# Hybrid encoder layer on one core: gate tiles stored from ScalarE's queue, a fourth row buffer, one rotary scratch per engine, and branch B's table arithmetic placed in a later phase

## The chip, the core and the metric

The kernel runs on one core of one Trainium2 chip. The metric is device microseconds of one execution, the median of several runs; lower is better. The core's engines are TensorE (PE in the profile), VectorE (DVE), ScalarE (ACT), GpSimd (POOL) and SyncE (SP). Each works through its own list of instructions in order and waits on semaphores. SP's list here holds only transfers (DMAs): it issues each one when its condition holds, and everything behind it on the list waits for that.

## The reference

One layer of an encoder, applied to two request groups (prompt and sample, 1024 tokens each, model width 1024) with the same weights:

```python
mod = silu(c) @ w_ada + b_ada;  shift, scale, gate = split(mod, 3)
h = rms_norm(x, norm_g) * (1 + scale) + shift
qa, ka, va, za, qb, kb, vb, zb, ga, gb = split(h @ w_in, ...)
# branch A: 8 q heads, 2 kv heads, width 64, RMSNorm of q and k, axial rotary positions
oa = gqa_attention(rope(norm(qa)), rope(norm(ka)), va) * silu(za)
# branch B: 4 heads, two softmax maps each, lambda from lam_q1, lam_k1, lam_q2, lam_k2
ob = rms_norm(diff_attention(rope16(norm(qb)), rope16(norm(kb)), vb, lam), subln_g) * (1 - lam_init)
pa = oa @ w_proj_a;  pb = (ob * silu(zb)) @ w_proj_b
merged = sigmoid(ga) * pa + sigmoid(gb) * pb
y = x + gate * (merged @ w_out)
```

Everything is float32.

## The kernel before, in words

Matrices are multiplied as high and low halves: `split_w` copies a weight tile into `w`'s high half on ACT (L209) and the difference into its low half on DVE (L210), and each product is three matmuls. The layer runs once for the prompt (group 0, the first 975 us or so) and once for the sample (group 1).

In each group the combined projection is cut in streams, written as Python generators: `kva_gen` (keys and values of A), `qa_gen` (queries of A, two halves), `vb_gen` and `qkb_gen` (branch B), and `z_gen`, which makes the gate paths: per 128 x 512 tile 24 matmuls (L900), a tanh from the PSUM bank into the single buffer `ev` (`z_out`, L882), and a store of `ev` to DRAM (L887). Tiles of za and zb are "gated": DVE forms silu in `ev` (L884) before the store. Tiles of ga and gb, 32 of the 48 in each group, are not. Because `ev` has one buffer, the next tile's tanh waits until the store has landed.

Rows of q and k (128 tokens) go through `rows`: ACT copies PSUM into a `row` buffer (`rtile`, three of them) and squares it, DVE sums, POOL takes the power. `rope` turns them: cos product into a scratch `rc` (L728; one buffer for both engines), two sin products (L737), a sum that reads `rc` (L738). `by_turns` gives even tiles to DVE and odd ones to POOL while `alone` or `easy` holds, else all to POOL. `pairs_T` transposes the rows on PE (L749) and evacuates the bank by ACT (L751) and DVE (L752).

Attention runs in steps: scores (L927 and L928) into one of two double banks, maximum on DVE (L929), exponential on ACT (L931), transposition of 32 x 32 blocks on DVE (L972), four SP transfers that finish it (`q<-p`, L977), and the product with V (L1003 in A, L1040 in B). `swapped` loads the turned halves of q (`sw<-u`, L783).

`weave` sets the order in which the streams are written down: it always takes the stream whose done share, less a constant, is least. The shares and constants are the tables at the top (`ATT_W`, `IN_A`, `Z_A`, `GATE_A`, `FIRST_A`, `Z_FIRST_A`, `LATE_A`). A scheduler then places the instructions on the engines by priority; `dma_next` and `in_order` keep the order of the program.

Group 0's head computes modulation, normalised input and first projections. `gate_gen` forms the adaLN gate in two halves (its matmuls on L110 read `cpad`, in the `at` scratch; ACT L625, PE L629, DVE L631). When the head is done, `load_tables_B` loads the rotary tables of branch B, its gains, the four lambda vectors and `subg`, and does all arithmetic on them (L581 to L600) before the first attention is written down. At a group's end `gated_gen` loads a piece of attention output and of z into two `row` buffers (L1146, L1147), multiplies them (L1152 or L1156, L1160) and splits the product (L1161, L1162); then come `merge_gen` (L1189 matmuls) and `out_gen` (L1220 matmuls).

Of the kernel before, what the change touches and what calls it, by code (L numbers as in the profile page):

```python
# [20 lines left out]
P = 128  # L21
T = 1024
D = 1024
NCH = D // P
NTT = T // P
HD = 64
EPS = 1e-6
LAM_INIT = 0.8 - 0.6 * math.exp(-0.3 * 0)
# [12 lines left out]
Z_HEAD = (7, 6)  # L41
Z_HEAD_A = (-0.216, -0.32)
ATT_W = (
    (0.733, 1.008, 0.894, 1.192, 1.03, 1.769),
    (1.237, 1.862, 1.041, 1.418, 0.645, 1.256),
)
IN_A = (
    (0.044, -0.07, 0.861, 0.05, 0.25, 0.15),
    (0.125, -0.05, 0.368, 0.3, -0.03, 0.694),
)  # L50
Z_A = (
    (0.2, 0.05, 0.62, -0.05, -0.1, -0.05),
    (-0.215, 0.07, 0.2, 0.16, -0.3, -0.1),
)
LAST_ATT = (46, 40)
LAST_FILL = (20, 25)
GATED_A = (0.063, -0.144)
LATE_A = 1.202
EARLY_A = 0.9
QUARTER_P = 202  # L60
KV_STEPS = 12
GATE_A = (-0.778, -0.677)
FIRST_ATT = 12
FIRST_A = 0.357
TAIL = (3, 3)
TAIL_A = (0.92, 1.2)
# [47 lines left out]
def kernel(ctx: ExitStack, tc: tile.TileContext, t: dict):  # L114
    nc = tc.nc
    ent = ctx.enter_context

    const = ent(tc.tile_pool(name="const", bufs=1))
# [47 lines left out]
    def ptile():  # L166
        return ppool.tile([P, 1024], F32, tag="p", name=nm("p"))
# [10 lines left out]
    def mtile(tag, shape, dt=F32, bufs=None):  # L178
        return mpool.tile(shape, dt, tag=tag, name=nm(tag), bufs=bufs)

    def rtile():
        return mtile("row", [P, 512], bufs=3)

    dma = nc.sync.dma_start
    act, vec, pe = (in_order(tc, e) for e in (nc.scalar, nc.vector, nc.tensor))
# [101 lines left out]

    ccol = const.tile([P, NCH, 2], F32, name="ccol")  # L290
    bcol = const.tile([P, 3, NCH], F32, name="bcol")
    gcol = const.tile([P, NCH], F32, name="gcol")
# [167 lines left out]

    def start(ht):
        still = rtile()[:, :256]
        nc.vector.memset(still, 0.0)
        cpad = mtile("at", [P, 256], bufs=1).rearrange("p (c m) -> p c m", c=NCH)
        nc.vector.memset(cpad, 0.0)
        nc.scalar.activation(cT, ccol, AF.Tanh, scale=0.5)
        nc.vector.scalar_tensor_tensor(out=cT, in0=cT, scalar=1.0, in1=ccol, op0=ALU.add, op1=ALU.mult)
        nc.vector.tensor_scalar(out=cT, in0=cT, scalar1=0.5, scalar2=None, op0=ALU.mult)
        nc.vector.tensor_copy(cpad[:, :, :2], cT)
        xT = [load_xT0(0)]  # L470
        wts = [load_ada(n) for n in range(2)]
# [24 lines left out]
        rsb = spread(rs, pe)
        idle(WARM[3], still[:, :128])
        vec.tensor_scalar(out=bcol[:, 1, :], in0=bcol[:, 1, :], scalar1=1.0, scalar2=None, op0=ALU.add)
        part = ada_part(ada_half(wts[1], cpad, 1, first))
        early.update({n: four_sums() for n in range(2)})  # L500
        ps = ada_sum(part)
        idle(WARM[4], still[:, :128])
        with tc.high_priority(offset=QUARTER_P):
            for quarter in range(4):
                cs = range(quarter * 2, quarter * 2 + 2)
                if quarter % 2 == 0:
                    add_h(ht, 0, quarter // 2)
# [12 lines left out]
                for c in cs:  # L520
                    sums_early(ht, c, 0)
                part = ada(wts[quarter * 2 + 2 : quarter * 2 + 4], cpad) if quarter < 3 else None
                for c in cs:
                    sums_early(ht, c, 1)
                    if part is not None:
                        ps, part = ada_sum(part), None
        kva_w.append((drain_last(z_first),))
        sq = late_squares(xT[1])
        return lambda: inv_rms(sq, pe), lambda rs: start_late(ht, xT[1], rs), gate_gen(cpad)
# [14 lines left out]
            if c % 2:  # L544
                yield 1

    cosB = const.tile([P, 2, NTT, 16], F32, name="cosB")
    sinB = const.tile([P, 2, NTT, 16], F32, name="sinB")
    gqa = const.tile([P, HD], F32, name="gqa")
    gka = const.tile([P, HD], F32, name="gka")  # L550
# [19 lines left out]
    def load_tables():  # L570
        for dst, src in ((gqa, "qn_a"), (gka, "kn_a")):
            dma_next(dst, t[src][0].partition_broadcast(P))
        nc.vector.tensor_scalar(out=gqa, in0=gqa, scalar1=SC, scalar2=None, op0=ALU.mult)

    def load_tables_B():
        for dst, src in ((cosB, "cosB"), (sinB, "sinB")):
            for a in range(2):
                dma_next(dst[:, a], t[src].rearrange("(n p) d -> p n d", p=P))
        for i, src in enumerate(("qn_b", "kn_b")):
            dma_next(gB[:, i, :], t[src][0].partition_broadcast(P))  # L580
        nc.vector.tensor_scalar(out=gB[:, 0, :], in0=gB[:, 0, :], scalar1=SC, scalar2=None, op0=ALU.mult)  # L581
        for a in range(2):
            by_q(cosB[:, a], sinB[:, a], gB[:, a], 8)

        nc.vector.tensor_tensor(out=gB[:, 0, 16:], in0=gB[:, 0, 16:], in1=gB[:, 1, 16:], op=ALU.mult)

        lamw = ptile()
        lamv = lamw[:, : 4 * HD].rearrange("p (a d) -> p a d", a=4)
        for i, src in enumerate(("lam_q1", "lam_k1", "lam_q2", "lam_k2")):
            dma_next(lamv[:, i, :], t[src][0].partition_broadcast(P))  # L590
        lamp = lamw[:, 4 * HD : 6 * HD].rearrange("p (a d) -> p a d", a=2)
        nc.vector.tensor_tensor(
            out=lamp, in0=lamv[:, 0::2, :], in1=lamv[:, 1::2, :], op=ALU.mult
        )
        nc.vector.tensor_reduce(out=lam2, in_=lamp, axis=AX.X, op=ALU.add)
        nc.scalar.activation(lam2, lam2, AF.Exp)
        nc.vector.tensor_tensor(out=nlam, in0=lam2[:, 1:2], in1=lam2[:, 0:1], op=ALU.subtract)
        nc.vector.tensor_scalar(out=nlam, in0=nlam, scalar1=-LAM_INIT, scalar2=None, op0=ALU.add)
        dma_next(subg, t["subln_g"].rearrange("o e -> e o"))
        nc.vector.tensor_scalar(out=subg, in0=subg, scalar1=0.5 * (1.0 - LAM_INIT) * math.sqrt(2 * HD), scalar2=None, op0=ALU.mult)  # L600

    def load_tables_A(st):

# [113 lines left out]
    def rope(x3, s3, cos, sin, half, e):  # L717

        nh, w = x3.shape[1], x3.shape[2]
        c3 = mtile("rc", [P, 4, HD], bufs=1)[:, :nh, :w]  # L720
        k, g = cos.shape[1], w // (2 * half)
        if k == 1:
            cs = cos.to_broadcast([P, nh, w])
# [156 lines left out]
    def z_out(dst, key, ps, gated):  # L880
        ev = mtile("ev", [P, 512], bufs=1)
        nc.scalar.activation(ev, ps, AF.Tanh, scale=0.5)  # L882
        if gated:
            nc.vector.scalar_tensor_tensor(out=ev, in0=ev, scalar=1.0, in1=ps, op0=ALU.add, op1=ALU.mult)  # L884
        dt = dpool.tile([P, 512], F32, name=nm("zd"))
        dst[key] = dt
        dma(dt, ev)  # L887

    def z_gen(ht, col, dst, i0, gated, w=None, hfs=(0, 1)):
        w = w or load_w(w_cols(w_in, (col, 256)))  # L890
# [131 lines left out]
    def b_values(u):  # L1022
# [20 lines left out]
        else:  # L1043
# [6 lines left out]
                pv(*ready.pop(0))  # L1050
                yield 1
            pv(*ready.pop())
        sq = mtile("at", [P, 256], bufs=1)
        o = mtile("oo", [P, 256])
        nc.scalar.activation(query_order(sq), piece_order(acc), AF.Square)
        nc.vector.tensor_copy(query_order(o), piece_order(acc))
# [283 lines left out]
    for g in range(2):  # L1340
        st = states[g]
# [5 lines left out]
        zs = chain(*items)  # L1347
        qa = head(g, st, zs, late)
        alone[0] = False
        if g == 0:  # L1350
            load_tables_B()

        att = attention(units_of(st), qa)

# [8 lines left out]
        if g == 0:  # L1363
            weave((islice(att, FIRST_ATT), FIRST_ATT, 0.0), (qa, 15, FIRST_A), (islice(zs, Z_FIRST[1]), Z_FIRST[1], Z_FIRST_A[1]))
        easy[0] = True
        phase(0, qa_gen(st, 1))
        phase(1, vb_gen(ht, st["vb"], 0), qkb_gen(ht, st["qkb"], 0))
        easy[0] = False
        oT, mT = ([], []), ([], [])
# [85 lines left out]
```

## Time and profile before

| | |
|---|---|
| median of 3 runs | 1889.12 us (1887.71 to 1893.15) |
| the profiled execution | 1889.37 us, its span 1887.3 us |
| PE busy | 1853.1 us, 98% of the span |
| DVE, ACT, POOL busy | 1229.1, 845.5, 362.7 us |
| transfers | 297.51 MB, all through one queue that SP issues |

The span runs from the first to the last instruction; the 2.07 us between it and the execution's time lie outside the trace. PE's busy time counts pipelined matmuls from issue to end, so a busy PE can still be slower than it could be; idle time on PE is a loss without doubt. In a row of instructions, "[2.97 <-DVE u L752]" means that the engine stood idle for 2.97 us before it and that DVE's instruction of line 752, writing tile u, ended the wait.

### The profile page before, as it was taken

Reading aid. Unit: us, or ns where it says so; the run is one execution under the profiler, and the core shown is the slowest. Engines: PE = TensorE matmul, PEld = TensorE weight load, DVE = VectorE, ACT = ScalarE, POOL = GpSimd, SP = SyncE. Lnnn points to the kernel's source line nnn. Section 1 sums busy time; section 2 is a strip of 40 time slices with the busy share of each in tenths; the row PEclk is TensorE's granted clock in tenths of the full one; section 3 lists DMA queues with packets and bytes.
Section 4 is the critical chain, followed back from the end, with each engine's and each line's share of the span. In section 5 each row is a group of like instructions: output and inputs, shape, how many; then the busy total and the mean of one; then the engine's idle time right before and its main releaser. Section 6 shows DMA issues by size and latency. Waiting matters only on the chain.

```text
span 1887.3 us, 32062 instructions
## 1 busy us (share of the span) xinstructions
PE 1853.1 (98%) x11484; PEld 1602.5 (85%) x11484; DVE 1229.1 (65%) x1892; ACT 845.5 (45%) x1803; POOL 362.7 (19%) x692
## 2 busy tenths in 40 slices
PE   9989999999999999999999999999999999999999
PEld 7768888888889998778889888888888989877887
DVE  4746686646578678778464777666547766787731
ACT  3524454445456555424223555444445545552210
POOL 0422210011325152100124300000233513210000
PEclk9999999999999999999999999999999999999999
DMA  9525567665444436887541477766524344579532
GB/s 332 166 62 145 131 177 182 175 162 136 134 126 102 129 90 183 238 291 225 199 134 46 123 185 190 205 177 181 153 78 125 99 104 114 154 239 303 168 106 78
DMA packets 277612, 299.54 MB, mean 159 GB/s; under 512 B 37648, under 2 KB 228304, under 8 KB 277456
## 3 DMA queue, kind: packets, MB, share of 16 engines
q1 hardware_dynamic: 277456, 297.51, 55.4%
q8 instruction: 92, 1.51, 0.3%
q14 instruction: 64, 0.52, 0.1%
HBM read 137.91 MB, written 42.04 MB: 95 GB/s over the span
## 4 chain that ended last, share of the span: by engine, by line
PE 76%; DMA 7%; DVE 6%; SPq 4%; ACT 2%; POOL 2%; issue 2%; DVEq 0%; ACTq 0%; POOLq 0%
PE f L900 20%; PE f L689 19%; PE a L1003 6%; PE f L1220 5%; PE f L1189 5%; PE s L927 5%; PE s L928 5%; PE a L1040 4%; PE s L1220 4%; PE s L1189 2%; SPq L977 2%; SPq L110 2%; DMA st<-in_w_in_dram 1%; DVE m L929 1%; DMA row<-zd 1%
## 5 line engine op out<-in xcount | busy, mean ns | idle before, releaser
L900 PE MATMUL f<-u,w 128*128 128x512 f32 x2064 | 518.8, 394 | 0.9 <-ACT ev L882 0.3
L689 PE MATMUL f<-w,u 128*128 128x256 f32 x3264 | 451.3, 287 | 0.5 <-ACT ev L882 0.3
L900 PEld LDWEIGHTS f<-u,w 128*128 128x128 f32 x2064 | 379.3, 188 | 76.9 <-ACT ev L882 0.8
L689 PEld LDWEIGHTS f<-w,u 128*128 128x128 f32 x3264 | 428.0, 192 | 17.3 <-issue 0.7
L929 DVE TENSOR_REDUCE m<-s 128x1 f32<-128x1024 f32 x256 | 310.2, 1219 | 140.4 <-PE s L928 138.0
L972 DVE STREAM_TRANSPOSE p<-p 128x1024 f32<-128x1024 f32 x192 | 238.4, 1242 | 53.6 <-ACT p L931 47.8
L928 PE MATMUL s<-u,sw 128*128 128x512 f32 x512 | 202.8, 399 | 0.0
L210 DVE TENSOR_TENSOR w<-st,w 128x512 fp32r<-128x512 f32 x184 | 124.6, 707 | 88.5 <-ACT w L209 87.7
L209 ACT ACTIVATE w<-st 128x512 fp32r<-128x512 f32 x184 | 108.2, 626 | 125.1 <-DMA st<-in_w_in_dram 58.6
L931 ACT ACTIVATE p<-s,m,rsB 128x1024 f32<-128x1024 f32 x128 | 154.2, 1205 | 4.1 <-DMA q<-p 0.6
L931 ACT ACTIVATE p<-s,m,rsA 128x1024 f32<-128x1024 f32 x128 | 154.3, 1205 | 3.9 <-ACT m L930 0.4
L714 POOL TENSOR_TENSOR rsB<-ss,nhalf 128x4 f32<-128x4 f32 x64 | 66.4, 1037 | 426.2 <-DVE ss L713 415.8
L1189 PE MATMUL f<-u,w 128*128 128x512 f32 x588 | 142.5, 392 | 0.9 <-DVE u L1200 0.5
L1040 PE MATMUL a<-q,u 128*128 128x256 f32 x512 | 126.5, 390 | 7.9 <-DMA q<-p 4.6
L1189 PEld LDWEIGHTS f<-u,w 128*128 128x128 f32 x588 | 109.9, 188 | 24.5 <-DVE u L1200 0.9
L1003 PE MATMUL a<-q,u 128*64 128x128 f32 x2048 | 121.6, 277 | 3.4 <-DMA q<-p 3.4
L1003 PEld LDWEIGHTS a<-q,u 128*64 128x64 f32 x2048 | 113.0, 138 | 13.2 <-issue 6.5
L752 DVE TENSOR_TENSOR u<-f,u 64x256 fp32r<-64x256 f32 (+1 forms) x210 | 84.9, 406 | 56.2 <-ACT u L751 50.7
L1040 PEld LDWEIGHTS a<-q,u 128*128 128x128 f32 x512 | 97.4, 196 | 23.3 <-issue 5.8
L928 PEld LDWEIGHTS s<-u,sw 128*128 128x128 f32 x512 | 97.0, 189 | 16.6 <-issue 0.3
L927 PE MATMUL s<-u 128*128 128x512 f32 x256 | 107.5, 422 | 1.1 <-ACT p L931 0.9
L1220 PE MATMUL f<-u,w 128*128 128x512 f32 x456 | 105.3, 389 | 0.0
(205 smaller groups left out, 2162.7 us busy)
## 6 DMA issues: line engine op xcount, KB each, us to landing
q<-p SPq DMA_DIRECT2D x768, 128.0 KB, 2.8
st<-in_w_in_dram SPq DMA_DIRECT2D x128, 256.0 KB, 3.3
zd<-ev SPq DMA_DIRECT2D x96, 256.0 KB, 2.3
sw<-u SPq DMA_DIRECT2D x256, 64.0 KB, 2.1
p<-zd SPq DMA_DIRECT2D x64, 256.0 KB, 4.6
u<-in_w_ada_dram SPq DMA_DIRECT2D x24, 512.0 KB, 8.5
od<-oo SPq DMA_DIRECT2D x64, 128.0 KB, 2.6
st<-in_w_in_dram SPq DMA_DIRECT2D x64, 128.0 KB, 2.8
```

The source lines that it names most:

```text
L210: nc.vector.tensor_tensor(out=wl, in0=st, in1=wh.bitcast(F32), op=ALU.subtract)
L689: nc.tensor.matmul(ps, lt[c][:, sl], w[c][:, wi, :], start=(k == 0), stop=(k == 23))
L900: nc.tensor.matmul(ps, w[c][:, wi, e * P : (e + 1) * P], rt[c], start=(k == 0), stop=(k == 23),)
L927: nc.tensor.matmul(s[:, sl], q, k[:, sl], start=True, stop=False)
L928: nc.tensor.matmul(s[:, sl], sw, k[:, sl], start=False, stop=True)
L929: nc.vector.tensor_reduce(out=m, in_=s, axis=AX.X, op=ALU.max, negate=True)
L931: nc.scalar.activation(pt.rearrange("p (j c a) -> p j c a", j=4, c=8), s.rearrange("p (c a j) -> p j c a", c=8, j=4), AF.Exp, scale=rs, bi ...
L972: nc.vector.transpose(pt, pt)
L1003: nc.tensor.matmul(acc[e * 64 : e * 64 + 64, n * P : n * P + P], u["v"](k), blocks[n][:, e, k], start=(k == 0 and n == 1), stop=(k == 7 an ...
L1040: nc.tensor.matmul(acc, u["v"][:, k], pT[:, k], start=(k == 0), stop=(k == 7))
L1189: nc.tensor.matmul(ps, w[:, c, wi, d * P : (d + 1) * P], o[:, oi, :], start=(k == 0), stop=(k == 11))
L1220: nc.tensor.matmul(ps, w[c][:, wi, e * P : (e + 1) * P], m[:, mi, :], start=(k == 0), stop=(k == 23))
```

## The change

What it does, part by part:

- `z_out` issues the store of an ungated tile (ga, gb) from ACT; the gated tiles' stores stay on SP.
- `rtile` has four buffers.
- `rope` takes its scratch by engine: `rcv` on DVE, `rcg` on POOL, one buffer each. The squares of branch B's output (`sq` in `b_values`) move from `at` to `rcv`, and `at` is gone. `cpad` moves into the room of `cosB`.
- The lambda vectors are loaded in `load_tables`, into an `oo` buffer; their product and sum (`lambdas`) run with `folded`. `load_tables_B` becomes a generator: its loads are issued where they were, its arithmetic is four later steps woven into phase 0 (the second half of qa and most of A's first attention half).
- Eight constants of the weave change and TABLES_A is new; all of them bear on group 0 alone.

```diff
-    (0.733, 1.008, 0.894, 1.192, 1.03, 1.769),
+    (0.826, 1.008, 0.894, 1.192, 1.03, 1.769),        # ATT_W[0]
-    (0.044, -0.07, 0.861, 0.05, 0.25, 0.15),
+    (0.044, -0.07, 0.891, 0.05, 0.25, 0.15),          # IN_A[0]
-    (0.2, 0.05, 0.62, -0.05, -0.1, -0.05),
+    (0.099, 0.05, 0.62, -0.05, -0.1, -0.05),          # Z_A[0]
-LATE_A = 1.202
+TABLES_A = 0.0
+LATE_A = 1.25
-GATE_A = (-0.778, -0.677)
+GATE_A = (-0.778, -0.875)
-FIRST_A = 0.357
+FIRST_A = 0.073
-Z_FIRST_A = (-0.035, -0.317)
+Z_FIRST_A = (-0.093, -0.181)
...
-        return mtile("row", [P, 512], bufs=3)
+        return mtile("row", [P, 512], bufs=4)
...
-        cpad = mtile("at", [P, 256], bufs=1).rearrange("p (c m) -> p c m", c=NCH)
+        cpad = cosB.rearrange("p a n d -> p (a n d)").rearrange("p (c m) -> p c m", c=NCH)
...
+        lamv = mtile("oo", [P, 256]).rearrange("p (a d) -> p a d", a=4)
+        lams.append(lamv)
+        for i, src in enumerate(("lam_q1", "lam_q2", "lam_k1", "lam_k2")):
+            dma_next(lamv[:, i, :], t[src][0].partition_broadcast(P))
+
+    def lambdas():
+        lamv = lams.pop()
+        lamp = lamv[:, :2]
+        nc.vector.tensor_tensor(out=lamp, in0=lamp, in1=lamv[:, 2:], op=ALU.mult)
+        nc.vector.tensor_reduce(out=lam2, in_=lamp, axis=AX.X, op=ALU.add)
...
-    def load_tables_B():
+    def tables_B_gen():
...
         for i, src in enumerate(("qn_b", "kn_b")):
             dma_next(gB[:, i, :], t[src][0].partition_broadcast(P))
+        dma_next(subg, t["subln_g"].rearrange("o e -> e o"))
+        yield 1
         nc.vector.tensor_scalar(out=gB[:, 0, :], in0=gB[:, 0, :], scalar1=SC, ...)
-        for a in range(2):
-            by_q(cosB[:, a], sinB[:, a], gB[:, a], 8)
+        by_q(cosB[:, 0], sinB[:, 0], gB[:, 0], 8)
+        yield 1
+        by_q(cosB[:, 1], sinB[:, 1], gB[:, 1], 8)
         nc.vector.tensor_tensor(out=gB[:, 0, 16:], in0=gB[:, 0, 16:], in1=gB[:, 1, 16:], op=ALU.mult)
+        yield 1
+        nc.vector.tensor_scalar(out=subg, in0=subg, scalar1=..., op0=ALU.mult)
+        yield 1
         nc.scalar.activation(lam2, lam2, AF.Exp)
         nc.vector.tensor_tensor(out=nlam, in0=lam2[:, 1:2], in1=lam2[:, 0:1], op=ALU.subtract)
         nc.vector.tensor_scalar(out=nlam, in0=nlam, scalar1=-LAM_INIT, scalar2=None, op0=ALU.add)
+        yield 1
...
-        c3 = mtile("rc", [P, 4, HD], bufs=1)[:, :nh, :w]
+        c3 = mtile("rcv" if e is nc.vector else "rcg", [P, 4, HD], bufs=1)[:, :nh, :w]
...
-        dma(dt, ev)
+        (dma if gated else nc.scalar.dma_start)(dt, ev)
...
-        sq = mtile("at", [P, 256], bufs=1)
+        sq = mtile("rcv", [P, 4, HD], bufs=1).rearrange("p a d -> p (a d)")
...
             by_q(st["cosA"], st["sinA"], gqa, 16)
+            if g == 0:
+                lambdas()
...
-        if g == 0:
-            load_tables_B()
+        tables = [tables_B_gen()] if g == 0 else []
+        for gen in tables:
+            next(gen)
...
-        phase(0, qa_gen(st, 1))
+        phase(0, qa_gen(st, 1), more=[(gen, 4, TABLES_A) for gen in tables])
```

More of the change, by code (lines that the diff above doesn't have):

```diff
@@ L285, in load_w_proj @@
         return w
+    cosB = const.tile([P, 2, NTT, 16], F32, name="cosB")
     ccol = const.tile([P, NCH, 2], F32, name="ccol")
@@ L545, in start_late @@
                 yield 1
-    cosB = const.tile([P, 2, NTT, 16], F32, name="cosB")
     sinB = const.tile([P, 2, NTT, 16], F32, name="sinB")
@@ L573, in load_tables @@
         nc.vector.tensor_scalar(out=gqa, in0=gqa, scalar1=SC, scalar2=None, op0=ALU.mult)
-    def load_tables_B():
+        lamv = mtile("oo", [P, 256]).rearrange("p (a d) -> p a d", a=4)
[7 more added lines that the diff above has]
+        nc.vector.tensor_reduce(out=lam2, in_=lamp, axis=AX.X, op=ALU.add)
+    lams = []
+    def tables_B_gen():
         for dst, src in ((cosB, "cosB"), (sinB, "sinB")):
@@ L580, in load_tables_B @@
             dma_next(gB[:, i, :], t[src][0].partition_broadcast(P))
+        dma_next(subg, t["subln_g"].rearrange("o e -> e o"))
+        yield 1
         nc.vector.tensor_scalar(out=gB[:, 0, :], in0=gB[:, 0, :], scalar1=SC, scalar2=None, op0=ALU.mult)
-        for a in range(2):
-            by_q(cosB[:, a], sinB[:, a], gB[:, a], 8)
+        by_q(cosB[:, 0], sinB[:, 0], gB[:, 0], 8)
+        yield 1
+        by_q(cosB[:, 1], sinB[:, 1], gB[:, 1], 8)
         nc.vector.tensor_tensor(out=gB[:, 0, 16:], in0=gB[:, 0, 16:], in1=gB[:, 1, 16:], op=ALU.mult)
[L587 to L595, printed above, removed]
+        yield 1
+        nc.vector.tensor_scalar(out=subg, in0=subg, scalar1=0.5 * (1.0 - LAM_INIT) * math.sqrt(2 * HD), scalar2=None, op0=ALU.mult)
+        yield 1
         nc.scalar.activation(lam2, lam2, AF.Exp)
@@ L598, in load_tables_B @@
         nc.vector.tensor_scalar(out=nlam, in0=nlam, scalar1=-LAM_INIT, scalar2=None, op0=ALU.add)
-        dma_next(subg, t["subln_g"].rearrange("o e -> e o"))
-        nc.vector.tensor_scalar(out=subg, in0=subg, scalar1=0.5 * (1.0 - LAM_INIT) * math.sqrt(2 * HD), scalar2=None, op0=ALU.mult)
+        yield 1
     def load_tables_A(st):
```

## The prediction, as written before the run

> **What bounds the kernel now.** I read the page's busy line first, then the cores, then the stretches in time, then PE's waits, and last the order of time around the longest ones.
>
> ```profile
> PE 1853.1 (98%) x11484; PEld 1602.5 (85%) x11484; DVE 1229.1 (65%) x1892; ACT 845.5 (45%) x1803; POOL 362.7 (19%) x692
> core 0: 1887.3 us, clock 0.993
> ```
>
> PE is the bound: it is idle for 1887.3 - 1853.1 = 34.2 us. The granted clock of 0.993 says that 0.007 x 1887.3 = 13 us of clock went missing too. What this change can win is in these two sums, since no matmul is added or removed. The stretches show where the idle time lies (columns: stretch, PE busy, PEld, DVE, ACT, POOL, granted clock, DMA share, GB/s):
>
> ```profile
> 60.00:95.00 35.00, 31.99 (x176) 25.61 (x175) 24.28 (x63) 15.38 (x40) 19.95 (x29) 1.00 0.52 181
> 120.00:142.00 22.00, 14.97 (x68) 11.24 (x67) 12.21 (x39) 8.14 (x24) 3.48 (x7) 0.87 0.39 100
> 142.00:260.00 118.00, 118.00 (x843) 103.94 (x842) 82.79 (x120) 58.84 (x131) 27.14 (x39) 0.98 0.56 146
> 260.00:300.00 40.00, 36.51 (x267) 30.54 (x265) 30.54 (x36) 22.26 (x47) 3.69 (x5) 1.00 0.72 184
> 760.00:830.00 70.00, 65.71 (x285) 53.69 (x285) 56.15 (x80) 28.30 (x54) 5.52 (x12) 0.95 0.82 243
> 1075.00:1320.00 245.00, 245.00 (x1859) 211.32 (x1860) 170.33 (x186) 124.69 (x253) 12.13 (x17) 1.00 0.70 184
> 1700.00:1795.00 95.00, 92.07 (x407) 76.08 (x407) 69.49 (x111) 26.53 (x48) 3.45 (x8) 0.98 0.70 230
> ```
>
> Group 0's head loses 3.0 us (60 to 95) and 7.0 us (120 to 142), its first attention 3.5 us, the end of its attention 4.3 us, that of group 1 2.9 us. Between them PE is full. PE's own waits name the releasers (total us, times, longest):
>
> ```profile
> PE f L749 <- DVE ev L884: 4.9, 1, 4.9
> PE a L1040 <- DMA q<-p: 4.6, 3, 2.7
> PE f L749 <- DVE u L752: 3.8, 2, 3.0
> PE a L1003 <- DMA q<-p: 3.4, 2, 2.5
> PE s L927 <- ACT p L931: 1.1, 2, 0.9
> ```
>
> **The change part by part.** All terms are against the profiled execution, 1889.37 us (span 1887.3 and 2.07 outside), which is 0.25 us above the median of 1889.12.
>
> *The tables of branch B.* In order of time on DVE, ACT and PE around 132 us:
>
> ```profile
> 135.32 0.29 DVE L592 TENSOR_TENSOR p<-p 128x128 f32<-128x128 f32 x1 [2.21 <-DMA p<-in_lam_k_dram]
> 136.02 0.15 DVE L600 TENSOR_SCALAR subg<-subg 128x1 f32<-128x1 f32 x1 [0.41 <-DMA subg<-in_subln_g_dram]
> 136.41 0.20 ACT L596 ACTIVATE lam<-lam 128x2 f32<-128x2 f32 x1 [8.57 <-DVE lam L595]
> 136.63 0.60 ACT L882 ACTIVATE ev<-f 128x512 f32<-128x512 f32 x1
> 137.26 0.69 DVE L884 SCALAR_TENSOR_TENSOR ev<-ev,f 128x512 f32<-128x512 f32 x1 [0.27 <-ACT ev L882]
> 125.77 5.76 PE L900 MATMUL f<-u,w 128*128 128x512 f32 x24 [0.31 <-ACT row L625]
> 132.07 1.03 PE L629 MATMUL f<-two,row 128*128 128x2 f32 x8 [0.43 <-DVE u L752]
> 138.01 1.73 PE L749 MATMUL f<-ident,p 128*128 128x128 f32 x6 [4.91 <-DVE ev L884]
> ```
>
> DVE waits in its list for tables that have just been asked for; ACT stands at the lambda exponential behind it; the tanh of the z tile, done on PE at 125.77 + 5.76 = 131.53, starts at 136.63, and PE waits 4.91 us for its bank. Without the tables the tanh can start at 131.5, DVE follow at 132.1 and free the bank at 132.8, before L629 ends at 133.1. The whole 4.91 us goes. The arithmetic comes back in phase 0, on a DVE that is 82.79 of 118 us busy there (142 to 260): eleven instructions of 0.15 to 0.29 us, as in the rows of L592 and L600, under 3 us in all. That cover is real only while PE waits for nothing on DVE; if it fails, it costs those 3 us. The lambda loads move ahead, to about 49 us, and put four small issues into SP's list ahead of weights; none of PE's waits above is for weights, so I take 0, and at worst the 1.5 us of four issues at a store's 0.356 us (row below).
>
> *The clock after a wait.* PE's rows in order of time give the same 24 matmuls of L689 at two places, and the stretches the clock:
>
> ```profile
> 95.27 4.63 PE L689 MATMUL f<-w,u 128*128 128x256 f32 x24 [0.30 <-ACT ev L882]
> 155.40 2.88 PE f L689 x24
> 142.29 3.84 PE f L689 x18
> 300.17 2.13 PE L1003 MATMUL a<-q,u 128*64 128x128 f32 x17 [2.52 <-DMA q<-p]
> 95.00:98.00 3.00, 2.73 (x13) 2.74 (x14) 2.78 (x8) 1.07 (x5) 1.75 (x3) 0.57 0.22 87
> 138.00:146.00 8.00, 7.20 (x29) 5.88 (x30) 4.10 (x12) 3.08 (x9) 0.00 (x0) 0.50 0.35 98
> 300.00:303.00 3.00, 2.83 (x27) 2.86 (x29) 2.72 (x4) 1.61 (x4) 0.00 (x0) 0.53 0.20 50
> ```
>
> After each wait PE runs at about half its clock for 3 us or more. At 95.27 that costs 4.63 - 2.88 = 1.75 us. At 142.29 it costs 3.84 - 18/24 x 2.88 = 1.68 us; what it costs between 138 and 142 I leave out, since evacuations by DVE pace that stretch anyway. So each removed wait gives 1.7 us besides itself.
>
> The Trainium skill ("TensorE: Matmul & The Clock Gate", The HAM clock gate) says that the clock is halved after an idle window of about 3.4 us. By that rule the 4.91 us wait would lose the clock and the 2.97 us one below might not, and the sum would be 1.7 us smaller. The rows differ: after the 2.52 us of idling that ended at 300.17 the granted clock was 0.53.
>
> *One rotary scratch per engine.* The other wait in the head:
>
> ```profile
> 88.74 0.28 DVE L738 TENSOR_TENSOR p<-rc,p 128x128 f32<-128x128 f32 x1
> 92.75 0.42 DVE L728 TENSOR_TENSOR rc<-p,tab 128x256 f32<-128x256 f32 x1 [3.73 <-POOL p L738]
> 93.67 0.28 DVE L752 TENSOR_TENSOR u<-f,u 64x128 fp32r<-64x128 f32 x1
> 94.64 0.33 PE L749 MATMUL f<-ident,p 128*128 128x128 f32 x1 [2.97 <-DVE u L752]
> ```
>
> DVE's next cos product can't be written until POOL's sum has read the shared `rc`; DVE idles 3.73 us, and behind it in its list stands the evacuation L752 that PE's transposes wait for. With `rcv` DVE goes on at 89.0, and the evacuation comes at about 93.67 - 3.73 = 89.9 or soon after, before PE runs dry at 94.64 - 2.97 = 91.7. PE's 2.97 us go, and the 0.30 us before the L689 of 95.27, whose ACT wait stands behind the same evacuation: 3.3 us, and 1.7 us of clock. What is late next is POOL's own chain; if it takes over, half is left. The Trainium skill ("SBUF — State Buffer", Who interferes with whom) says that a DVE instruction with two inputs in SBUF and a GpSimd one that reads SBUF block each other, and with own scratches the two ropes will overlap; by it some products would take 0.4 in place of 0.3 us, as the 0.42 us row may already show, and the sum would be under 0.5 us worse.
>
> *Stores from ACT's queue.* 64 of the 96 stores move. Rows of SP's list and of its waits:
>
> ```profile
> L887 SPq DMA_DIRECT2D zd<-ev x96: 319/356/652, 62.7 to 1696.8; - x96
> SPq L887 <- ACT ev L882: 86.9, 28, 15.9
> SPq L256 <- DMA st<-in_w_in_dram: 8.8, 10, 1.6
> 477.18 0.60 ACT L882 ACTIVATE ev<-f 128x512 f32<-128x512 f32 x1 [0.77 <-PE f L900]
> 479.99 5.14 SPq L977 DMA_DIRECT2D q<-p  x8
> 485.18 0.59 SPq L887 DMA_DIRECT2D zd<-ev  x1
> ```
>
> SP gets rid of 64 x 0.356 = 22.8 us of issues, and of waits for ACT during which `q<-p` and `sw<-u` stood behind. ACT takes the 22.8 us on: 845.5 becomes 868 us. Queued behind a store on ACT are exponentials, row copies and tanhs; PE waits for them. But PE's idle time ended by an exponential is 1.1 us over 256 scores, so ACT has room of a few us nearly everywhere, and 0.36 us more is mostly hidden. Bounds: PE's waits for `q<-p` are 4.6 + 3.4 = 8.0 us, so no more than that, with its clock, can come back; no ACT-issued transfer is in this trace, and if every store's issue fell on PE's path it would cost 22.8 us. I take 0, nearest to the 1.1 us row: 1 us lost at exponentials, 1 us won at `q<-p`.
>
> *A fourth row buffer.* It lets a second pair of `row` loads be asked for while a first is worked on. Such loads are waited for, though not by PE:
>
> ```profile
> DVE row L1156 <- DMA row<-zd: 10.3, 5, 4.6
> ```
>
> It can shorten the ends of attention, where PE loses 4.3 and 2.9 us, mostly to `q<-p`, which shares SP with these loads. Bounds 0 and 7.2 us; I take 0.5, nearest to 0, since PE's named wait there is another.
>
> *`sq` in `rcv`, `cpad` in `cosB`, the constants.* `sq` is written from phase 2 on, where all ropes run on POOL, so `rcv` is as free as `at` was: 0. The load of `cosB` now waits for the last reader of `cpad`; these are matmuls of the head, and the load is issued after them: 0. The constants reorder group 0's first phases, where PE idles 3.5 us (260 to 300) and nothing in group 1's like phase (1075 to 1320): so up to 3.5 us either way, 5 with the clock; I take 0.
>
> Sum: 4.9 + 1.7 (tables), 3.3 + 1.7 (scratch), 0.5 (rows): 12.1 us. 1889.37 - 12.1 = 1877.3; against the median, 1877.0 us.
>
> **The rivals.** Faster than that: SP, freed, ends the `q<-p` waits as well. All 8.0 us of them, less the 1 us taken above, and 1.7 us of clock behind each of the two longest (2.5 and 2.7 us): about 10 us, 1867. For it: SP issues back to back, eight transfers in 5.14 us. Against: the stores are 0.36 us each in these queues, and the end of attention is full of other loads.
>
> Within the measurement (0.3%, 5.7 us, is about what a measurement of this kernel can tell from no change): the reordered phase 0 opens waits of its own. Its attention is pushed harder (ATT_W 0.733 to 0.826), four `q<-p` of 0.6 us a step, and a wait like that at 297 costs 2.5 + 1.7 us. Two of them: 1877 + 8.4 = 1885. For it: the 260 to 300 row; against: 1075 to 1320.
>
> Slower: ACT stands at its stores as SP stood. SP's L256 row shows that an issue can wait for an earlier transfer's landing; the tile of 477.78 was stored at 485.18, since SP was late. If ACT has to wait for SP's transfers ahead of it, exponentials behind it wait too. From 12.1 + 5.7 = 17.8 us on PE, 0.28 us at each of 64 stores, it is slower; at 0.36 us each, 23 us, it is 1900. The Trainium skill ("Perfetto Trace Analysis", DMA Instruction — HWDGE) has one descriptor generator locked by each issuing sequencer in turn, which would make ACT's issue wait for SP's too; no row here can show it.
>
> **How the numbers follow.** The forecast has 0.55 (1872 to 1882 by itself); the freed SP 0.14; new waits 0.23; ACT 0.08. Faster by over 0.3% is 0.55 + 0.14 = 0.69, same 0.23, slower 0.08. The range runs from the freed SP's 1867 to 1889, the new waits' upper part; it leaves out 0.07 below and 0.1 above.
>
> **What would show it.** No tables between the head's last tile and PE's first transposes of qa, clock 1.0 there, and the first attention about 6 us earlier after the scratch's 5; no DVE wait for POOL's L738 at L728; stores as ACT's own transfers, near 0.36 us each, and PE's idle time ended by L931 still near 1 us. Wrong would be: PE idle above 26 us, new waits for L752, L884 or `q<-p` in group 0 before 435 us, or ACT's stores above 0.7 us.

## The result and the profile after

The changed kernel takes 1878.59 us (median of 6 runs, 1874.51 to 1880.69) against 1888.93 us for the kernel before, measured beside it: a ratio of 0.9945 with a 95% interval of 0.9931 to 0.9959, some 10 us less. The time forecast, 1877.0 us, is met. The reasons given for it are not, for the larger part, as the experiments show.

Line numbers are 1 higher in the first functions and 7 higher from `gate_gen` on (L110 is now L111, L882 L889, L884 L891, L927 L934, L1003 L1010, L1189 L1196); the experiments' kernels have shifts of their own, so that a line is best known by its tiles. L111, L110 in the kernel before, is the line of the wrapper that issues whatever is held in the order of the program. The page's busy line and the core's line of the kernel after:

```profile
PE 1850.2 (99%) x11484; PEld 1597.7 (85%) x11484; DVE 1229.3 (65%) x1892; ACT 845.1 (45%) x1803; POOL 371.2 (20%) x692
core 0: 1877.5 us, clock 0.995
```

The span is 9.8 us shorter. 6.9 us of it are idle time of PE (34.2 before, 1877.5 - 1850.2 = 27.3 now), 2.9 us are busy time, of which the clock is the part that can be named. The stretches after (PE busy, PEld, DVE, ACT, POOL, granted clock, DMA share, GB/s), and ahead of them two of before that the prediction didn't show:

```profile
0.00:60.00 60.00, 56.07 (x388) 46.17 (x389) 32.84 (x63) 27.73 (x47) 1.72 (x7) 1.00 0.91 286
300.00:435.00 135.00, 134.83 (x1048) 119.21 (x1049) 78.80 (x95) 62.33 (x127) 8.33 (x16) 0.99 0.65 170
```

```profile
0.00:60.00 60.00, 55.39 (x376) 44.73 (x377) 29.11 (x61) 26.23 (x44) 1.71 (x7) 0.97 0.91 287
60.00:95.00 35.00, 34.49 (x195) 28.02 (x194) 30.05 (x73) 17.66 (x47) 19.64 (x28) 1.00 0.53 183
120.00:142.00 22.00, 19.48 (x121) 15.14 (x121) 13.32 (x36) 9.22 (x23) 5.90 (x10) 1.00 0.38 82
142.00:260.00 118.00, 117.58 (x875) 102.87 (x874) 89.90 (x127) 63.70 (x140) 27.48 (x39) 1.00 0.64 163
260.00:300.00 40.00, 39.58 (x300) 33.69 (x300) 30.18 (x32) 22.30 (x44) 0.00 (x0) 1.00 0.70 181
760.00:830.00 70.00, 66.19 (x295) 54.71 (x295) 52.56 (x78) 23.95 (x47) 8.00 (x13) 0.98 0.86 270
```

Read against before: 60 to 95 gains 2.5 us of idle time, 120 to 142 gains 4.5 us and the clock, 142 to 260 gains 0.02 x 118 = 2.4 us of clock, 260 to 300 gains 3.1 us. The first 60 us lose: 0.7 us of idle time, and 0.03 x 60 = 1.8 us of clock. That clock is missing from 12 to 20 us (granted 0.83 and 0.74), well ahead of the new wait at 57 us. In the kernels below it is 0.97 over the first 60 us with the stores back on SP and 1.00 with three row buffers, so no run ties it to a part of the change. PE's waits after:

```profile
PE f L1196 <- ACT row L1139: 3.8, 1, 3.8
PE s L934 <- DVE m L936: 3.4, 1, 3.4
PE f L1196 <- DVE p L1202: 2.6, 1, 2.6
PE s L111 <- DVE u L111: 2.4, 2, 1.5
PE s L934 <- ACT p L938: 1.3, 2, 0.8
PE a L1010 <- DMA q<-p: 0.7, 2, 0.4
```

The long waits of the head for L752 and L884 are gone (for these two PE now waits at most 0.6 us at a time), and `q<-p` has gone from 4.6 + 3.4 us to 0.7. In their place stand two long waits at the ends of the two attentions (before 772 and 1692 us), one in the merge behind the first (before 847 us), and one early in the head. In order of time on DVE and PE, the early one, and the place to which the tables' arithmetic has gone:

```profile
57.16 0.29 DVE L583 TENSOR_TENSOR oo<-oo 128x128 f32<-128x128 f32 x1 [3.81 <-DMA oo<-in_lam_k_dram]
58.71 2.54 PE L111 MATMUL s<-w,u 128*128 128x256 f32 x19 [1.54 <-DVE u L111]
...
128.71 0.20 DVE L596 TENSOR_SCALAR gB<-gB 128x64 f32<-128x64 f32 x1 [4.13 <-DMA gB<-in_qn_b_dram]
128.94 0.29 DVE L562 TENSOR_TENSOR cosB<-cosB,gB 128x128 f32<-128x128 f32 x1
130.60 0.44 PE L756 MATMUL f<-ident,p 128*128 128x128 f32 x2 [0.57 <-DVE gatec L638]
```

The arithmetic was written down in steps of phase 0, but the scheduler placed it where its priority allowed: still in the head, 4.13 us of DVE behind tables that have just been asked for. The product of the lambdas, whose loads moved ahead, is at 57 us: DVE stands 3.81 us at a load, PE waits 1.54 us behind it. The stores:

```profile
L894 ACTq DMA_DIRECT2D zd<-ev x64: 326/326/365, 64.7 to 1684.3; - x64
L894 SPq DMA_DIRECT2D zd<-ev x32: 323/529/584, 132.2 to 1287.8; - x32
```

Last, the end of the first attention, ACT, then PE:

```profile
771.33 0.63 ACT L284 ACTIVATE w<-st 128x512 fp32r<-128x512 f32 x1 [4.18 <-DMA st<-in_w_proj_a_dram]
772.35 1.19 PE L1196 MATMUL f<-u,w 128*128 128x512 f32 x2 [3.81 <-ACT row L1139]
```

ACT stands at a weight load of the next stage, and the row copy that PE waits for is queued behind it. The wait for L936 before 1692 us has the same beginning: ACT's L284 stands 3.46 us at a load of the same weights, until 1689.42, and the exponential queued behind it ends at 1691.47, 0.1 us before the maximum that the profile names.

How much earlier than in before PE starts the same matmul, in us, worked out from PE's rows in order of time (one profiled execution each; the kernels are those of the experiments below):

| kernel | first score | 129th matmul of L928 (A's attention nearly done) | first L1189 | first L1220 | group 1's first score | end |
|---|---|---|---|---|---|---|
| after | 8.4 | 14.6 | 11.8 | 9.7 | 9.8 | 9.8 |
| constants alone | 4.0 | 10.7 | 8.6 | 11.4 | 11.4 | 11.5 |
| scratch alone | 3.9 | 5.5 | 5.1 | 5.5 | 5.5 | 5.7 |
| tables alone | 1.5 | 2.7 | 1.8 | 3.6 | 3.6 | 2.6 |
| after, old constants | 7.7 | 7.0 | 5.9 | 6.2 | 6.3 | 6.5 |
| after, old tables | 7.4 | 13.3 | 11.3 | 10.6 | 10.7 | 9.1 |
| after, tables held in order | 11.9 | 17.1 | 14.5 | 17.2 | 17.3 | 16.2 |

In the kernel after, 8.4 us are won in the head, 6.2 us in A's attention, and 5 us of these are given back by the end of group 0. Group 1 changes nothing. Of the 6.4 us by which the version with the tables held in order ends ahead of the kernel after, 2.5 us are there when A's attention is nearly done; the rest is that it gives nothing back by the first L1220.

### The profile page after: what moved, and what is told of

Read it like the earlier page. It is cut to its first block, busy times and chain, and to the rows that moved or that the text cites. A ratio compares the mean times of both kernels' runs of the same rounds, so it can differ in the third digit from the quotient of the medians.

```text
span 1877.5 us, 32041 instructions
## 1 busy us (share of the span) xinstructions
PE 1850.2 (99%) x11484; PEld 1597.7 (85%) x11484; DVE 1229.3 (65%) x1892; ACT 845.1 (45%) x1803; POOL 371.2 (20%) x692
## 4 chain that ended last, share of the span: by engine, by line
PE 77%; DVE 7%; DMA 6%; SPq 4%; issue 3%; ACT 2%; POOL 2%; DVEq 0%; ACTq 0%; POOLq 0%
PE f L907 20%; PE f L696 17%; PE f L1196 6%; PE a L1010 6%; PE f L1227 6%; PE s L934 5%; PE s L935 5%; PE a L1047 4%; PE s L1227 4%; PE s L1196 2%; SPq L984 2%; SPq L111 2%; DVE m L936 2%; DMA st<-in_w_in_dram 1%; DMA q<-p 1%
## 5 line engine op out<-in xcount | busy, mean ns | idle before, releaser
L907 PE MATMUL f<-u,w 128*128 128x512 f32 x2064 | 519.4, 394 | 1.0 <-DVE u L759 1.0
L936 DVE TENSOR_REDUCE m<-s 128x1 f32<-128x1024 f32 x256 | 309.7, 1218 | 136.6 <-PE s L935 134.6
L1196 PE MATMUL f<-u,w 128*128 128x512 f32 x588 | 145.4, 398 | 6.4 <-ACT row L1139 3.8
L1196 PEld LDWEIGHTS f<-u,w 128*128 128x128 f32 x588 | 111.9, 192 | 30.9 <-ACT row L1139 4.2
L1047 PE MATMUL a<-q,u 128*128 128x256 f32 x512 | 124.9, 384 | 0.0
L1010 PE MATMUL a<-q,u 128*64 128x128 f32 x2048 | 120.5, 274 | 1.0 <-DMA q<-p 0.7
L1010 PEld LDWEIGHTS a<-q,u 128*64 128x64 f32 x2048 | 111.7, 137 | 10.7 <-issue 8.7
L934 PE MATMUL s<-u 128*128 128x512 f32 x256 | 109.1, 428 | 4.8 <-DVE m L936 3.4
L1047 PEld LDWEIGHTS a<-q,u 128*128 128x128 f32 x512 | 96.1, 192 | 13.8
L758 ACT ACTIVATE u<-f 64x256 fp32r<-64x256 f32 (+1 forms) x210 | 75.7, 362 | 68.7 <-PE f L756 40.2
```

Of the source, the lines that this page charges most:

```text
L907: nc.tensor.matmul(ps, w[c][:, wi, e * P : (e + 1) * P], rt[c], start=(k == 0), stop=(k == 23),)
L934: nc.tensor.matmul(s[:, sl], q, k[:, sl], start=True, stop=False)
L936: nc.vector.tensor_reduce(out=m, in_=s, axis=AX.X, op=ALU.max, negate=True)
L1010: nc.tensor.matmul(acc[e * 64 : e * 64 + 64, n * P : n * P + P], u["v"](k), blocks[n][:, e, k], start=(k == 0 and n == 1), stop=(k == 7 an ...
L1047: nc.tensor.matmul(acc, u["v"][:, k], pT[:, k], start=(k == 0), stop=(k == 7))
L1196: nc.tensor.matmul(ps, w[:, c, wi, d * P : (d + 1) * P], o[:, oi, :], start=(k == 0), stop=(k == 11))
```

## The experiments

The theory under test was the prediction's sum: tables and scratches bring the time, the rest nothing. Its rivals were that the constants bring it, and that the freed SP does. Each part was undone in the kernel after, and four were done alone in the kernel before.

| kernel | median us | ratio to before | interval |
|---|---|---|---|
| after | 1878.59 | 0.9945 | 0.9931 to 0.9959 |
| after, stores on SP | 1881.05 | 0.9959 | 0.9947 to 0.9972 |
| after, one scratch for both engines and `sq` | 1904.46 | 1.0077 | 1.0062 to 1.0091 |
| after, one scratch, `sq` apart | 1879.09 | 0.9954 | 0.9941 to 0.9967 |
| after, three row buffers | 1878.42 | 0.9942 | 0.9927 to 0.9957 |
| after, old tables | 1877.62 | 0.9937 | 0.9923 to 0.9951 |
| after, old constants | 1882.70 | 0.9969 | 0.9957 to 0.9981 |
| scratch alone | 1884.74 | 0.9980 | 0.9971 to 0.9989 |
| tables alone | 1889.77 | 1.0011 | 1.0001 to 1.0022 |
| stores alone | 1890.69 | 1.0013 | 1.0002 to 1.0025 |
| constants alone | 1878.01 | 0.9952 | 0.9938 to 0.9966 |
| after, tables held in order | 1873.26 | 0.9919 | 0.9905 to 0.9933 |
| after, lambda product alone held in order | 1878.55 | 0.9950 | 0.9937 to 0.9963 |

The medians of before beside these lie between 1887.2 and 1889.1 us, so the ratios are what is compared. The intervals reach some 0.13% either way, so two ratios tell kernels apart from about 0.2%, 3.8 us, on (an estimate from these intervals). Among the undone parts only the constants and the shared scratch pass that, and so do the tables held in order. The placing of `cpad` in `cosB` was neither undone nor tried alone.

**The stores, undone.**

```diff
-        (dma if gated else nc.scalar.dma_start)(dt, ev)
+        dma(dt, ev)
```

> The changed kernel with all z stores issued by SP again. My theory: the moved stores were worth about nothing (1 us lost on ACT, 1 us won on SP), so 1878.6 us within 2.5 us, and PE's idle time in the head (60 to 142) as in the changed kernel, about 3 us. Rival: the 3.1 us of PE idle time that left the first attention (260 to 300, 3.5 to 0.4 us), with its lost clock, left because SP was freed; then that idle time comes back as waits for q<-p of 2 us or more and the time is 1883 us or above.

2.5 us slower in the medians, with overlapping intervals. PE is busy for 39.70 of the 40 us from 260 to 300, as in the kernel after (39.58): the `q<-p` waits that went there were not SP's stores. Elsewhere some come back: PE's waits for `q<-p` are 3.6 us in all against 0.7, 3.0 us of them at L1047, at the ends of the attentions. So the freed SP may be worth up to these 2.5 us there; the noise leaves it open.

**The stores alone**, the same line in the kernel before.

> The kernel before with the ungated stores issued by ACT and nothing else. The prediction's term: 0, 1889 us within 2.5 us (medians of before in these runs lay at 1888 to 1889 us). Rival, from the undone stores (2.5 us worse): the single ev buffer comes free earlier in the head, where PE waited 1.7 us at 83 us for an ACT copy behind a tanh; 2 to 3 us, 1886 us.

1.0013: no gain. PE's wait for `q<-p` at L1003 is 5.2 us (3.4 before), at L1040 3.4 us (4.6 before). An ACT issue takes 0.326 us, at most 0.364, so ACT does not stand at them either. PE's waits for exponentials do grow, from 1.1 to 3.7 us, by one of 3.5 us at 1700 us; ahead of that one ACT stands 3.45 us at a weight load (L283). In place of before's wait of 2.9 us for L958 at 1704 us stands one of 1.9 us for `q<-p`. The Trainium skill ("DMA: Bandwidth & Descriptors", Issuing engines are not separate DMA queues) says that transfers begun on several engines save no more than the sequencer's time to begin them; this pair of runs agrees.

**One scratch again.**

```diff
-        c3 = mtile("rcv" if e is nc.vector else "rcg", [P, 4, HD], bufs=1)[:, :nh, :w]
+        c3 = mtile("rcv", [P, 4, HD], bufs=1)[:, :nh, :w]
```

> The changed kernel with one rotary scratch for both engines. My theory: DVE's cos product waits for POOL's sum again near 92 us, PE loses about 3.3 us there and 1.7 us to the clock behind it, so 1883.6 us (1882 to 1886). Rival: with the new order in the head something else covers or replaces that wait, and the time stays at 1878.6 us within 2 us.

Some 25 us slower than the kernel after by the ratios. This was not the undoing that it was meant to be: `sq` lies in `rcv` in the kernel after, so here three engines share one buffer: ACT with `sq`, DVE and POOL with their ropes. Two rows of that tile (times of the first and the last at the end), and PE's largest wait:

```profile
L1062 ACT ACTIVATE rcv<-a x32: 363/376/388, 529.4 to 1742.7; 128x256 f32<-128x256 f32 x32
L735 POOL TENSOR_TENSOR rcv<-row,cosB x56: 317/323/1231, 400.6 to 1627.8; 128x64 f32<-128x64 f32 x56
```

```profile
PE s L934 <- ACT p L938: 10.5, 10, 3.9
```

POOL's ropes of branch B and ACT's squares overlap in time from 529 us on. Up to there the kernel is 1.1 us behind the kernel after; in group 1 it is 7.8 us behind at the end of A's attention, and the 129th product of B with V (L1047) of that group comes 31.7 us later. PE's waits for exponentials grow from 1.3 to 10.5 us. The way from the shared buffer to these waits was not followed row by row; that the sharing is the cause is shown by the next kernel.

**One scratch again, `sq` in a buffer of its own** (the line above, and this one).

```diff
-        sq = mtile("rcv", [P, 4, HD], bufs=1).rearrange("p a d -> p (a d)")
+        sq = mtile("at", [P, 256], bufs=1)
```

> The changed kernel with one rotary scratch for both engines, but the squares of branch B's output in a tile of their own, as before. The first undoing of the scratch (1904.5 us) put POOL's ropes and these squares into one buffer, which neither kernel does. My theory: that sharing was its 26 us, and here only the 2.7 us wait near 92 us and 1.7 us of clock come back: 1882 to 1884 us. Rival: one scratch for both engines itself costs 20 us or more in the new order: 1898 us or above.

0.9954: 0.5 us by the medians, 1.7 by the ratios, within the noise. A wait of 2.50 us is back at 95 us and the first score is 3.4 us later than in the kernel after, but at the first L1220 only 1.8 us of that are left.

**The scratch alone**, in the kernel before.

> The kernel before with one rotary scratch per engine and nothing else (the squares stay in at). My theory: the 2.97 us wait at 92 us and its clock go, 5 us: 1884 us (1882.5 to 1885.5), the wait of 4.9 us at 132 us stays. Rival: what the scratch frees is taken back by the wait at 132 us, which is set by the tables' loads and not by the work before: then PE's wait there grows from 4.9 to about 9 us and the time stays near 1888 us.

0.9980, 3.8 us by the ratio. PE's wait of 2.97 us at 91 us is now 0.97 us and ended by POOL's p of L806; the clock from 95 to 120 us is 1.00 (0.93 before). The wait at 132 us stays whole (129 to 134 us here).

**Three row buffers.**

```diff
-        return mtile("row", [P, 512], bufs=4)
+        return mtile("row", [P, 512], bufs=3)
```

> The changed kernel with three row buffers. My theory: 0.5 us, so 1879.1 us within 2 us, since PE waits for other things at the ends of attention. Rival: the fourth buffer is what lets gated_gen's loads run ahead, and the two ends of attention (PE idle 3.8 and 1.6 us in the changed kernel) lose 3 us or more: 1882 us or above.

0.9942: no gain in time that can be measured. It does change what PE waits for from 740 to 890 us. In this kernel PE waits 1.8 us for `q<-p` there and 3.6 us in all; in the kernel after nothing for `q<-p`, but 3.8 us for L1139 and 2.6 us for L1202. The other traces split the same way: the six kernels with three buffers wait 1.5 to 4.5 us for `q<-p` there and at most 0.9 us for the row of L1139, the eight with four wait at most 0.9 us for `q<-p` and 1.3 to 3.8 us for that row.

**The old tables**, lambda vectors and one piece after the head, in the kernel after.

```diff
-        tables = [tables_B_gen()] if g == 0 else []
-        for gen in tables:
-            next(gen)
+        if g == 0:
+            load_tables_B()
...
-        phase(0, qa_gen(st, 1), more=[(gen, 4, TABLES_A) for gen in tables])
+        phase(0, qa_gen(st, 1))
```

> The changed kernel with branch B's tables and lambdas loaded and worked on in one piece after the head, as before. My theory: the 4.9 us wait near 132 us and 1.7 us of clock come back, and the 1.5 us that PE waits at 57 to 59 us for a weight split behind the lambda product (DVE L583, which waits 3.8 us for lam_k) goes, with some clock: net 4 to 5 us, 1882.6 to 1883.6 us. Rival: the reordered head, not the tables, removed the wait at 132 us; then no PE wait above 2 us comes back there and the time is 1878.6 us or less.

0.9937, no slower than the kernel after. The wait in the head returns, 127.5 to 131.5 us, with the clock at 0.84 from 120 to 142; the start has PE busy for 56.36 of 60 us at a clock of 1.00 (55.39 at 0.97). In these two executions the two nearly cancel: 1.0 us is left at the first score. The 1.8 us of clock in the start are no price of the tables, though, as said above.

**The new tables alone**, in the kernel before.

> The kernel before with the tables of branch B as in the changed kernel (early lambda loads, arithmetic as a generator) and nothing else. The prediction's term: 6.6 us, 1882.5 us. Rival, from the undone tables, which cost nothing: the arithmetic stays in the head, the lambda product adds a wait at 57 us, and the net is 0 to 3 us: 1886 to 1889 us.

1.0011: the term of 6.6 us is measured as nothing. DVE and PE at the place of the lambda product, and two stretches:

```profile
56.87 0.29 DVE L582 TENSOR_TENSOR oo<-oo 128x128 f32<-128x128 f32 x1 [3.91 <-DMA oo<-in_lam_k_dram]
58.42 2.77 PE L110 MATMUL s<-w,u 128*128 128x256 f32 x21 [1.22 <-DVE u L110]
```

```profile
0.00:60.00 60.00, 54.44 (x379) 44.33 (x380) 29.43 (x61) 26.33 (x45) 1.72 (x7) 1.00 0.91 289
120.00:142.00 22.00, 18.32 (x87) 14.15 (x84) 11.98 (x37) 8.62 (x24) 3.50 (x7) 0.93 0.41 102
```

3.35 us of idle time are won from 120 to 142, and 1.6 us lost before 60; further waits come at 83 us (1.6 us, ended by ACT's row of L631) and at 96 us. Of a head that should be 6.6 us shorter, 1.5 us are left at the first score.

**The old constants**, in the kernel after, as in the change's diff.

> The changed kernel with the constants of the kernel before (TABLES_A kept). My theory: the constants are worth about nothing, 1878.6 us within 2.5 us. Rival, from the undone tables (1877.6 us, so the tables' part is worth nothing by itself): the constants reorder the head (the second half of the adaLN gate later, fewer waits there) and the first attention, and are worth several us; then 1882 us or above, with PE idle time near 3 us back in 260 to 300.

1882.70: 4 us slower than the kernel after. Its head is as short (7.7 us won against 8.4), and all is lost in A's attention, where `q<-p` waits of 1.1 us before 256 and 2.4 us before 293 are back:

```profile
260.00:300.00 40.00, 37.57 (x266) 32.29 (x265) 27.91 (x32) 19.15 (x40) 2.19 (x4) 0.96 0.73 189
```

**The new constants alone**, in the kernel before.

> The kernel before with the changed kernel's constants and nothing else. The prediction's term: 0. Rival, from the undone constants (4.1 us worse, with waits for q<-p of 1.3 and 2.6 us back between 250 and 300 us): about 4 us, 1885 us, with PE idle under 1 us from 260 to 300, and the waits of 3.0 and 4.9 us in the head still there.

0.9952: the constants by themselves do what the whole change does. Its stretches, and PE's waits:

```profile
120.00:142.00 22.00, 17.22 (x102) 12.77 (x101) 10.86 (x38) 6.99 (x19) 3.66 (x8) 1.00 0.45 112
142.00:260.00 118.00, 118.00 (x890) 104.15 (x889) 89.44 (x125) 64.01 (x140) 28.11 (x40) 1.00 0.61 156
260.00:300.00 40.00, 39.23 (x280) 33.19 (x279) 31.52 (x36) 22.41 (x46) 2.55 (x4) 1.00 0.72 188
300.00:435.00 135.00, 134.72 (x1032) 118.38 (x1032) 78.42 (x99) 61.35 (x127) 8.79 (x17) 1.00 0.65 171
```

```profile
PE a L1041 <- DMA q<-p: 4.8, 3, 2.3
PE f L750 <- DVE u L753: 3.9, 2, 3.3
PE f L901 <- DVE u L753: 3.5, 2, 3.2
PE a L1004 <- DMA q<-p: 1.1, 2, 0.8
```

The wait that the scratch removes is still there (L750, 3.3 us). From 142 to 435 us the gain can be added up: idle time 3.66 us before, 1.05 us now, and clock 0.02 x 118 + 0.01 x 135 = 3.7 us before, none now; together 6.3 us, beside the 10.7 - 4.0 = 6.7 us of the markers. This profiled run has an unusually high clock, 0.999; over its five runs the median is 0.996, over 23 runs of before 0.994. By these two 0.002 x 1887 = 3.8 us of some 9 are clock.

**The tables held in order**, the version that the runs above point to: the kernel after, with the arithmetic of the tables and of the lambdas issued through the wrappers that keep the program's order, so that the scheduler can't pull it into the head.

```diff
-        nc.vector.tensor_scalar(out=gB[:, 0, :], in0=gB[:, 0, :], scalar1=SC, scalar2=None, op0=ALU.mult)
-        by_q(cosB[:, 0], sinB[:, 0], gB[:, 0], 8)
+        vec.tensor_scalar(out=gB[:, 0, :], in0=gB[:, 0, :], scalar1=SC, scalar2=None, op0=ALU.mult)
+        by_q_in(cosB[:, 0], sinB[:, 0], gB[:, 0], 8)
...
-        nc.scalar.activation(lam2, lam2, AF.Exp)
+        lambdas()
+        act.activation(lam2, lam2, AF.Exp)
...
-            if g == 0:
-                lambdas()
```

> The changed kernel with branch B's table arithmetic and the lambda product held in the order of the program, so that they really stand in phase 0 (in the changed kernel the lambda product stands at 57 us and the tables at 129 us). My theory: PE's 1.5 us wait at 57 to 59 us with its clock and the 0.6 us wait for DVE's gatec at 130 us go: 2 to 3 us, 1876 us. Rival: the head's end is set by the evacuations and PE loses the same elsewhere, or DVE's 3 us come back in phase 0: 1878.6 us or above.

1873.26 us, 0.9919: 5.3 us below the kernel after by the medians, 4.9 by the ratios, and the best here. The arithmetic now stands where it was written, between 138 and 249 us; three of its rows:

```profile
138.23 0.36 DVE L111 TENSOR_SCALAR gB<-gB 128x64 f32<-128x64 f32 x1
181.64 0.20 DVE L111 TENSOR_TENSOR gB<-gB 128x48 f32<-128x48 f32 x1
240.74 0.28 DVE L111 TENSOR_REDUCE lam<-oo 128x2 f32<-128x128 f32 x1
```

Its stretches:

```profile
0.00:60.00 60.00, 56.38 (x390) 46.48 (x391) 33.03 (x64) 27.70 (x47) 1.72 (x7) 1.00 0.91 289
120.00:142.00 22.00, 20.17 (x126) 17.64 (x127) 11.11 (x28) 7.83 (x19) 6.98 (x11) 1.00 0.42 92
142.00:260.00 118.00, 115.78 (x857) 100.85 (x856) 93.18 (x139) 65.91 (x146) 24.80 (x35) 1.00 0.64 166
```

Both losses in the head are gone, 1.8 us of them the clock from 12 to 20 us that no part accounts for, and the first score is 11.9 us earlier than in before. Of the 6.3 us between its span and that of the kernel after, PE's idle time is 1.5 us (25.8 against 27.3) and its busy time 4.8 us: most of the gain is clock, 0.998 against 0.995 in the medians of the runs. The cover in phase 0 is not free: in this kernel PE waits once for the evacuation of `ev` on DVE, at 255 us:

```profile
257.66 0.72 PE L920 MATMUL f<-u,w 128*128 128x512 f32 x2 [2.07 <-DVE ev L904]
```

**The lambda product alone held in order**, the kernel after with `lambdas()` moved as above and the rest left.

> The changed kernel with only the lambda product held in the order of the program (phase 0); the tables' arithmetic stays where the scheduler puts it, at about 129 us. It splits the 5.3 us by which holding both won (1873.3 against 1878.6 us). Theory: the lambda product in front of a weight split at 57 us was worth PE's 1.5 us wait and the clock behind it, 2.5 to 3 us: 1875.6 to 1876.1 us. Rival: the early part of the head gives nothing at the end, and the whole 5.3 us came from the tables at 129 us or from the end of attention: 1878.6 us within 1.5 us.

0.9950: no gain in the medians, though the clock is 1.00 in the first 60 us of this execution and the first score 1.6 us earlier than in the kernel after. So the gain of holding both belongs to the tables' arithmetic, or to both together.

## Why the prediction was right in the number and wrong in its steps

The number came from 12.1 us in two parts of the change; the runs put most of the gain in a third, which the prediction had at zero. That the sum agreed is chance.

- *The tables, 4.91 + 1.7 us: wrong.* The step that failed is "The arithmetic comes back in phase 0". It took the place in the program for the place on the engine. Only what is written through the order-keeping wrappers stays where it is written; the rest was hoisted into the head, where its loads are late (4.13 us idle on DVE before 128.71). "The lambda loads move ahead ... I take 0" failed likewise: the loads cost nothing, but their first reader was hoisted after them to 57 us, and its wait stands ahead of the tile (`u` of L111) that PE waits for. The part measures 1.0011 alone and -0.08% when undone. What the early lambda loads did bring is that PE's wait behind the tables is 0.57 us in the kernel after against 4.05 us with the old tables; the product at 57 us stands against it. With the order held something of the forecast comes: against the old tables in the same kernel, which is the comparison that the 6.6 us were for, 4.4 us by the medians and 3.4 by the ratios, hardly clear of the noise.
- *The scratch, 3.3 + 1.7 us: mechanism right, size 3.8 us alone.* DVE no longer waits for POOL's sum, and the clock after it is 1.00. What is late next is POOL's chain, named as the half that might remain: 1.0 us of PE's wait are ended by it. In the kernel after, undoing it costs 0.5 us by the medians and 1.7 by the ratios: half of its 3.4 us in the head is not there at the end. The 0.42 us row says nothing of the two engines blocking each other: it is of a tile twice as wide as the 0.28 us row, and takes 0.43 us with own scratches too.
- *Constants, 0, "up to 3.5 us either way, 5 with the clock": the term that was mis-sized.* Alone they bring 9 us by the ratio, undone they cost 4.5 us. The rival that had them open new `q<-p` waits in phase 0 has the wrong sign: these went from 3.4 us at L1003 to 0.7 in the kernel after (1.1 alone). The prediction bounded them by the 3.5 us of one stretch. They also shorten the wait at 132 us, and with it the half clock that reached from there into 142 to 260 (0.98 before). Which of the eight constants does it was not tried.
- *Stores, 0: right within what can be measured* (+0.13% alone, 0.14% when undone, of opposite sign). ACT's issue is 0.326 us, and PE's waits for exponentials stayed at 1.3 us (1.1 before). Neither the 10 us of the freed SP nor ACT standing at its stores came true.
- *Row buffer, 0.5: right within what can be measured*, but the `q<-p` waits at the end of attention, which the prediction kept apart from it, do go with it; other waits take their place. *`sq`: right as written*, since `rcg` had freed `rcv`; the 25 us of the shared version show what stood behind that zero.
- *What would show it.* "PE idle above 26 us" did come, with 27.3: 3.81 + 3.4 + 2.6 us stand at the ends of the attentions and in the merge, where the kernel after waits for ACT's L1139, DVE's L936 and L1202. These were not among the steps. No wait above 0.6 us for the head's evacuations or for `q<-p` came before 435 us. Of the signs for it, tables still stand in the head (128.71), and the first score is 8.4 us earlier, not some 11; no DVE wait for POOL's sum, the clock of 1.00 from 120 to 142 and the stores near 0.36 us came as said.

The parts do not add: alone they are -0.48% (constants), -0.20%, +0.11% and +0.13%, undone in the kernel after they are +0.24%, +0.09%, -0.08% and +0.14%, the last three within the noise. Two parts that shorten the same head share one gain, and a part of it goes again at the end of group 0. The fourth row buffer has a share in that end's waits: without it PE waits 3.6 us from 740 to 890 us in place of 6.4. Why ACT's loads of the next weights come late there, and why the version held in order waits only 3.6 us with four buffers, stays open.

## What to carry to other kernels

Where a scheduler places instructions, "moved to a later phase" must be read from the engine's rows, not from the program; arithmetic on a fresh load is held in order, or it can be hoisted to stand at that load. Constants that set the order of streams deserve a term and bounds of their own, over all the stretches that they order, above all where one stretch in one group idles and its twin in the other group doesn't. A change of several parts is priced by undoing and by doing alone, since both together show what the parts share.

## What the runs showed of the hardware

The price of the clock after a wait is not fixed. The prediction took 1.7 us behind each wait. The rows of PE that end a wait of nearly the same length, and the stretch of 4 us behind each, first in the kernel with the scratch alone, then with the constants alone:

```profile
296.32 0.95 PE L1003 MATMUL a<-q,u 128*64 128x128 f32 x12 [2.60 <-DMA q<-p]
296.32:300.32 4.00, 4.00 (x65) 3.83 (x66) 2.47 (x4) 1.52 (x4) 0.00 (x0) 1.00 0.25 53
```

```profile
94.98 0.33 PE L750 MATMUL f<-ident,p 128*128 128x128 f32 x1 [3.34 <-DVE u L753]
94.98:98.98 4.00, 3.70 (x18) 3.51 (x19) 3.67 (x11) 1.43 (x5) 2.67 (x4) 0.64 0.17 66
128.54 0.70 PE L901 MATMUL f<-u,w 128*128 128x512 f32 x2 [3.25 <-DVE u L753]
128.54:132.54 4.00, 4.00 (x18) 3.29 (x19) 2.26 (x13) 0.29 (x2) 0.00 (x0) 1.00 0.47 148
```

After 2.60 us the clock is whole, where in before the same wait of 2.52 us left 0.53; within one kernel 3.34 us lose it and 3.25 us don't. The Trainium skill ("TensorE: Matmul & The Clock Gate", What's actually happening) has the activity window run freely, so that the moment of a transition varies; the spread here agrees with that, while the waits below its 3.4 us that lost the clock do not fit one whole idle window. Over all 14 traces PE waits 30 times for 2.5 to 3.4 us; in the 4 us behind, the granted clock is 0.50 to 0.69 for 21 of them and 1.00 for nine. Behind all ten longer waits it is 0.50 to 0.67. So a wait of 2.5 to 3.4 us costs the clock or not, and the mean clock differs from run to run: 0.993 to 0.999 over the five of the constants alone.
